# The opening of a diffusion trunk: the first norm's row by one product with ones, its root by logarithm and exponential, and another order of the first loads

## The chip, the cores and the metric

The kernel runs on one core of one Trainium2 chip. The metric is the device time of one execution in microseconds; three runs of the kernel before gave 2091.67, 2094.18 and 2094.89 us. A core has TensorE (PE; its weight loads are listed as PEld), VectorE (DVE), ScalarE (ACT), GpSimd (POOL) and SyncE (SP). Each works through its own list of instructions strictly in order, and they wait for each other through semaphores. Transfers are issued from a queue (SP's or ACT's) and run on 16 DMA engines that all queues share.

## The reference

One layer of a trunk over 1024 latent tokens of width 1024 and 256 context tokens: a SwiGLU block, a mixing block (retention and gated linear attention), a second SwiGLU block, and a last norm. What matters here is the start of the first block:

```python
def rms_norm(x, w):
    y = xf * lax.rsqrt(jnp.mean(xf * xf, axis=-1, keepdims=True) + EPS)
    return (y * w.astype(jnp.float32)).astype(x.dtype)
...
m_l = jnp.split(cond_lat @ ada_w[i] + ada_b[i], N_MOD, axis=-1)
x = x + 0.5 * m_l[2][:, None, :] * swiglu(modulate(rms_norm(x, norm1_w[i]), m_l[0], m_l[1]),
                                            ffn1_w1[i], ffn1_w3[i], ffn1_w2[i])
```

`cond_lat` is silu(c), `modulate(h, shift, scale)` is h * (1 + scale) + shift.

## The kernel before

**Layout.** Activations lie with the width on the partitions: x is 16 tiles `x{tg}{k}` of 128 x 512, k = 0..7 the slice of the width, tg = 0, 1 the half of the tokens. Every float32 product is made of three fast ones: each operand is split into a high part (a rounding copy, on ACT) and a low part (the difference, on DVE), and high x high, high x low and low x high are summed in PSUM. For the activation the parts are `hh` and `hl`; for a weight `wh`, `whi`, `s` (high) and `wl`, `wlo`, `s` (low).

**The opening** is written out by hand in `first1`: on PE, DVE and ACT the program order is the order of execution. It loads x's first half (`load_x`), then weights (`raw`, by `fetch`) and columns of the modulation matrix (`ada`, 128 x 1024, by `pe_load`), all on SP's queue. The constants `cols`, `ident` and `ccol` (the conditioning as columns, padded with zeros to blocks of 32) come through ACT's queue.

The norm needs, for each token, one over the root of the mean square, in the same row on every partition. Before: `squares` sums the eight squared tiles into `nacc` (squares on ACT, adds on DVE; `nsq` has two buffers); `rstd_col` multiplies `nacc` with ones on PE, which gives a column for each 128 tokens; `pow_half` takes the power -0.5 (a scale and shift on DVE, the power on GpSimd); `rows_diag` makes four diagonal matrices on DVE; `rstd_rows` multiplies ones with them on PE, which gives the row in PSUM (`pr`), and a copy `nrb`.

Each tile k also needs two columns of modulation: scale, number 8 + k, and shift, number k. In the opening the first few are made on PE: `pe_sums` (eight narrow products of `ccol` with an `ada` tile), a copy `csum` on ACT, `pe_turn` (a product that brings the partial sums to the partitions), and `pe_out` on ACT into `mod`; scale columns then pass `mod_fin` on DVE. The rest of the scale columns are sums of products on DVE (`mod_sum`, tile `junk`), with the conditioning spread to all partitions (`condc`), to which `cond_silu` applies silu on ACT.

With row and columns, tile k is normed: x times scale times row on DVE (`norm_a1`, or the first half of `norm_a`), `hh` on ACT with the shift (`norm_a2`), `hl` on DVE (`norm_b`).

**The steps.** Six weight blocks i = 0..5 are multiplied side by side. In step st (0 to 7) PE does three products for each block with tile k = st, 18 in all, and in between the column sum and turn for tile st + 1. While it does, ACT and DVE norm tile st + 1 and split further weights (`FIRST` says which in which step), SP loads the second half of x (`X1`), and ACT and DVE square and add it (`SQ`). In step 7 the second half's `rstd_col` comes, and soon after its row. Before the norm is ready, `warm` keeps PE busy with products of ones, in the numbers of `WARM`.

**Tables.** ACT's functions sit in sets that are loaded. At the start a silu on a small tile (`warm` in `run`) brings in the silu set.

Of the kernel before, what the change touches and what calls it, by code (L numbers as in the profile page):

```python
# [390 lines left out]
class Trunk:  # L391
# [36 lines left out]
    def consts(self):  # L428
        nc, I, cp = self.nc, self.I, self.cp
        self.cols = self.tile(cp, [P, I["cols"].shape[1]], F32, "cols")  # L430
        nc.scalar.dma_start(self.cols, I["cols"])
        self.pad(cp, 16)
# [5 lines left out]
        nc.vector.memset(self.mhalf, -0.5)  # L438
        self.mods = self.tile(cp, [P, 112], F32, "mod")
        self.mod = [self.mods[:, :72], self.mods[:, 72:]]  # L440
# [16 lines left out]
    def pe_cond(self, pool):  # L457
        nc = self.nc
        t = self.tile(pool, [P, 36 * KD], F32, "ccol")[:, :33 * KD]
        nc.scalar.dma_start(t, self.I["ccol"])  # L460
        self.sel = t[:, 32 * KD:32 * KD + 2]
        self.ccol = t[:, :32 * KD]
        nc.scalar.activation(self.ccol, self.ccol, AF.Silu)
# [669 lines left out]
    def first1(self, pools, n1):  # L1133
# [25 lines left out]
        def load(i, q):  # L1159
            low(i, q, high(i, q))  # L1160
# [21 lines left out]
        x0, x1 = self.x[0], None  # L1182
        self.ndg, idle, pss, acc = 4, self.psA(), {}, None
# [21 lines left out]
        self.norm_a(0, 0, a, b, pr, n1, x0[0])  # L1205
        rb[0] = self.scr(n1, "nrb")
        nc.scalar.copy(rb[0], pr)
        low(1, 0, raw)
        sm = self.pe_copy(pc, P, n1)
# [4 lines left out]
        o9 = self.pe_turn(rc, 4, sm[0])  # L1214
        for i in range(2):
            mms(i, 0, (1,))
        load(2, 0)
        self.pe_out(9, o9)
        load(3, 0)
        self.norm_a1(0, 1, a, rb[0], x0[1])  # L1220
        self.pe_sums(pc, P, cur[1])
        raw = high(4, 0)
        sm = self.tile(n1, [P, P], F32, "csum128", 2)
        nc.scalar.copy(sm, pc[:, P:2 * P])
        low(4, 0, raw)
        load(5, 0)
        cur = {}
# [3 lines left out]
        for i in range(2, 6):  # L1231
            if i == 4:
                o1 = self.pe_turn(rc, 6, sm)
                self.pe_out(1, o1)
                self.norm_a2(0, 1, b, x0[1])
            pss[i] = (self.psA if i < 4 else self.psB)()
            mms(i, 0, (0, 2, 1))
        self.norm_b(0, 1, b, x0[1])
        self.cond_silu()
        for st in range(1, KD):  # L1240
            n = st + 1
            for w in FIRST.get(st, ()):
                fetch(*w)
            if st in X1:
                self.load_x(pools, (1,), X1[st])
            if n + 2 < KD:
                cur[10 + n], cur[n + 2] = self.mod_load(10 + n), self.pe_load(n + 2)
            if st == KD - 2:
                w3 = [self.tile(self.dp, [P, D], F32R, f"ada{i}") for i in (1, 2, 3, 4)]
                ws += [[tuple(t[:, o:o + 512] for t in w3[j:j + 2]) for o in (0, 512)] for j in (0, 2)]  # L1250
            for i in range(6):
                mms(i, st, (0, 2, 1))
                if i == 0 and n < KD:
                    sm = sums(n, 0)
                    self.mod_sum(8 + n, cur.pop(8 + n), (0,), True)
                    self.norm_a1(0, n, a, rb[0], x0[n])
                if i == 2 and n < KD:
                    self.pe_out(n, self.pe_turn(pc, 2 * P, sm))
                    self.norm_a2(0, n, b, x0[n])
                    self.norm_b(0, n, b, x0[n])  # L1260
                    for w in FIRST.get(st, ()):
                        load(*w)
                    if st in SQ:
                        acc = self.squares(self.x[1], 512, n1, "", SQ[st], acc)
                if n == KD:
                    if i == 0:
                        self.c_silu(0, 0, pss[0], True)
                        load(6, 0), load(6, 1)
                    if i == 2:
                        r = self.rstd_col(acc, 512, n1)  # L1270
                        self.c_mul(0, 0, pss[1])
                        self.c_silu(1, 0, pss[2], True)
                    if i == 4:
# [25 lines left out]
    def load_x(self, pools, tgs, ks=tuple(range(KD))):  # L1299
        nc, I = self.nc, self.I  # L1300
        for tg in tgs:
            o, n = TGS[tg]
            self.x.setdefault(tg, [])
            for k in ks:
                t = self.tile(pools[tg], [P, n], F32, f"x{tg}{k}")
                src = I["xT"][k * P:(k + 1) * P, o:o + n] if tg < 2 else I["ctxT"][k * P:(k + 1) * P, :]
                nc.sync.dma_start(t, src)
                self.x[tg].append(t)
# [639 lines left out]
    def run(self):  # L1948
# [18 lines left out]
        warm = self.tile(self.dp, [P, 64], F32, "warm")[:, :8]  # L1967
        nc.scalar.activation(warm, self.mhalf, AF.Silu)
# [48 lines left out]
        for at, (tg, k) in zip(xat, ((tg, 4 * q + k) for tg, q in ((0, 0), (1, 1), (0, 1), (1, 0)) for k in range(4))):  # L2017
            o = TGS[tg][0]
            plan[at].append(lambda tg=tg, k=k, o=o: nc.sync.dma_start(self.x[tg][k], I["xT"][k * P:(k + 1) * P, o:o + 512]))
# [204 lines left out]
for _n, _w in (("ada_b", 72), ("norm1_w", 8), ("norm2_w", 8), ("norm3_w", 8), ("final_norm_w", 8),  # L2224
               ("ret_norm_w", 4), ("gla_norm_w", 4), ("gla_b", 4)):
# [9 lines left out]
def layout(inputs):  # L2235
# [3 lines left out]
    A["xT"] = c(g["x"][0].T)  # L2239
# [5 lines left out]
    A["ccol"] = np.zeros((P, 33 * KD), np.float32)  # L2245
    for i, n in enumerate(("c", "c_ctx")):
        A["ccol"][:, i:32 * KD:32] = g[n].reshape(KD, P).T
        A["ccol"][i::32, 32 * KD + i] = 1.0
# [69 lines left out]
```

## Time and profile before

| | us |
|---|---|
| median of three runs | 2094.18 |
| the profiled execution | 2095.94 |
| its span on the core | 2094.1 |
| TensorE busy | 2079.5 |
| VectorE busy | 1464.5 |
| ScalarE busy | 965.7 |
| GpSimd busy | 198.0 |
| start of the first product of hh with a weight | 18.66 |

A timeline row reads: start, duration (of all in the row, from the first's start to the last's end), engine, line, operation, output<-inputs, partitions x elements, how many, and in brackets the idle time just before and what ended it. A float32 product of 128 x 128 with ones shows as two records. A row of a table of stretches reads: stretch, length, then busy time and count of PE, PEld, DVE, ACT and POOL, TensorE's granted clock, the share of the DMA engines, GB/s. A row of waits names who waited for whom, the total, the number and the longest. PE's records overlap (each carries its pipeline's run-out), so the spacing of starts is the better measure there.

### The profile page before, as it was taken

Reading aid. Unit: us, or ns where it says so; the run is one execution under the profiler, and the core shown is the slowest. Engines: PE = TensorE matmul, PEld = TensorE weight load, DVE = VectorE, ACT = ScalarE, POOL = GpSimd, SP = SyncE. Lnnn points to the kernel's source line nnn. Section 1 sums busy time; section 2 is a strip of 40 time slices with the busy share of each in tenths; the row PEclk is TensorE's granted clock in tenths of the full one; section 3 lists DMA queues with packets and bytes.
Section 4 is the critical chain, followed back from the end, with each engine's and each line's share of the span. In section 5 each row is a group of like instructions: output and inputs, shape, how many; then the busy total and the mean of one; then the engine's idle time right before and its main releaser. Section 6 shows DMA issues by size and latency. Waiting matters only on the chain.

```text
span 2094.1 us, 34655 instructions
## 1 busy us (share of the span) xinstructions
PE 2079.5 (99%) x12646; PEld 1782.1 (85%) x12646; DVE 1464.5 (70%) x2649; ACT 965.7 (46%) x1806; POOL 198.0 (9%) x196
## 2 busy tenths in 40 slices
PE   9999999999999999999999999999999999999998
PEld 7888888888889999999789988888788888888888
DVE  6889999666775445863786368768766666665686
ACT  5433433435544445665664246444434334344552
POOL 0000000000015664001011001000000000010000
PEclk9999999999999999999999999999999999999999
DMA  9267767459886553663222223242344454477674
GB/s 347 86 232 236 241 219 253 151 164 367 287 293 217 181 182 103 207 207 91 88 76 85 76 81 104 91 161 81 106 160 140 144 170 156 148 237 231 219 241 142
DMA packets 199643, 366.54 MB, mean 175 GB/s; under 512 B 23216, under 2 KB 36400, under 8 KB 199472
## 3 DMA queue, kind: packets, MB, share of 16 engines
q1 hardware_dynamic: 199040, 364.07, 52.7%
q8 instruction: 99, 1.62, 0.3%
q14 instruction: 72, 0.59, 0.1%
q10 hardware_dynamic: 432, 0.26, 0.0%
HBM read 289.66 MB, written 66.19 MB: 170 GB/s over the span
## 4 chain that ended last, share of the span: by engine, by line
PE 89%; DVE 4%; DMA 4%; issue 1%; ACT 1%; SPq 0%; DVEq 0%; POOL 0%; POOLq 0%; ACTq 0%
PE psa L147 18%; PE psa L424 11%; PE psa L426 11%; PE psa L425 11%; PE psb L426 9%; PE psb L425 9%; PE psb L424 9%; PE psb L147 8%; DMA raw<-in_w 1%; PE psa L1174 1%; DVE wlo L420 1%; DMA hl<-sd 1%; PE psa L1168 1%; DVE junk L505 1%; DMA s<-in_w 1%
## 5 line engine op out<-in xcount | busy, mean ns | idle before, releaser
L419 ACT ACTIVATE whi<-raw 128x512 fp32r<-128x512 f32 x371 | 234.0, 631 | 504.0 <-issue 155.0
L420 DVE TENSOR_TENSOR wlo<-raw,whi 128x512 fp32r<-128x512 f32 x371 | 255.2, 689 | 175.3 <-ACT whi L419 174.6
L424 PE MATMUL psa<-hh,whi 128*128 128x512 f32 x684 | 266.8, 390 | 0.1
L425 PE MATMUL psa<-hl,whi 128*128 128x512 f32 x684 | 266.2, 389 | 0.0
L426 PE MATMUL psa<-hh,wlo 128*128 128x512 f32 x684 | 266.2, 389 | 0.0
L425 PE MATMUL psb<-hl,whi 128*128 128x512 f32 x568 | 221.3, 390 | 0.9 <-DVE hl L420 0.9
L426 PE MATMUL psb<-hh,wlo 128*128 128x512 f32 x568 | 221.2, 390 | 0.6 <-DVE wlo L420 0.6
L424 PE MATMUL psb<-hh,whi 128*128 128x512 f32 x568 | 221.2, 389 | 0.5 <-ACT whi L419 0.5
L147 PE MATMUL psa<-hl,whi 128*128 128x512 f32 x384 | 153.5, 400 | 0.0
L147 PE MATMUL psa<-hh,whi 128*128 128x512 f32 x384 | 152.5, 397 | 0.0
L147 PE MATMUL psa<-hh,wlo 128*128 128x512 f32 x384 | 152.4, 397 | 0.0
L424 PEld LDWEIGHTS psa<-hh,whi 128*128 128x128 f32 x684 | 128.4, 188 | 27.4 <-ACT s L720 0.6
L426 PEld LDWEIGHTS psa<-hh,wlo 128*128 128x128 f32 x684 | 128.3, 188 | 26.8 <-DVE wlo L420 0.2
L425 PEld LDWEIGHTS psa<-hl,whi 128*128 128x128 f32 x684 | 128.4, 188 | 26.2
L147 DVE TENSOR_TENSOR wlo<-raw,whi 128x512 fp32r<-128x512 f32 (+1 forms) x132 | 83.0, 645 | 93.4 <-ACT whi L147 91.2
L420 POOL TENSOR_TENSOR hl<-s,hh 128x512 fp32r<-128x512 f32 x88 | 132.2, 1529 | 144.7 <-DVE hl L420 80.7
L147 ACT ACTIVATE whi<-raw 128x512 fp32r<-128x512 f32 (+1 forms) x132 | 77.5, 598 | 121.5 <-PE psa L147 101.2
L425 PEld LDWEIGHTS psb<-hl,whi 128*128 128x128 f32 x568 | 106.6, 188 | 24.2 <-DVE hl L420 2.2
L426 PEld LDWEIGHTS psb<-hh,wlo 128*128 128x128 f32 x568 | 106.6, 188 | 23.5 <-DVE wlo L420 1.5
L424 PEld LDWEIGHTS psb<-hh,whi 128*128 128x128 f32 x568 | 106.6, 188 | 23.3 <-ACT whi L419 1.0
L426 PE MATMUL psa<-hh,hl 128*128 128x256 f32 x392 | 111.1, 284 | 0.0
L424 PE MATMUL psa<-hh,hh 128*128 128x256 f32 x392 | 111.1, 283 | 0.0
(414 smaller groups left out, 4919.5 us busy)
## 6 DMA issues: line engine op xcount, KB each, us to landing
raw<-in_w SPq DMA_DIRECT2D x242, 256.0 KB, 3.4
s<-in_w SPq DMA_DIRECT2D x198, 256.0 KB, 3.8
gd<-s SPq DMA_DIRECT2D x154, 256.0 KB, 2.8
ada<-in_adaT SPq DMA_DIRECT2D x60, 512.0 KB, 4.4
raw<-gd SPq DMA_DIRECT2D x91, 256.0 KB, 3.1
sd<-s SPq DMA_DIRECT2D x44, 256.0 KB, 2.7
raw<-sd SPq DMA_DIRECT2D x44, 256.0 KB, 3.4
hh<-in_w SPq DMA_DIRECT2D x44, 256.0 KB, 3.8
```

Of the source, the lines that this page charges most:

```text
L147: self.rec.add(self.eng, lambda: f(*map(get, a), **{x: get(v) for x, v in k.items()}), outs, ins, name, a, k)
L419: nc.scalar.activation(hi, src, AF.Copy)
L420: (eng or nc.vector).tensor_tensor(out=lo, in0=src, in1=hi.bitcast(F32), op=ALU.subtract)
L424: mm(ps, wa[0], xa[0], start=start, stop=False, skip_group_check=more)
L425: mm(ps, wa[0], xa[1], start=False, stop=False, skip_group_check=more)
L426: mm(ps, wa[1], xa[0], start=False, stop=stop, skip_group_check=more)
L505: nc.vector.tensor_tensor_reduce(out=self.junk, in0=t, in1=self.cs[s], scale=1.0, scalar=self.col("ada_b")[:, j:j + 1], op0=ALU.mult, op1= ...
L1168: nc.tensor.matmul(idle[:, :P], self.ones, self.ones, start=True, stop=True)
L1174: nc.tensor.matmul(pss[i], w[u], h[v], start=k == 0 and j == 0, stop=k == KD - 1 and j == js[-1])
```

## The change

Six things change, all before step 7 ends.

- The row of the first norm is one product of a matrix of ones with `nacc`, 512 wide, which leaves each token's sum on every partition. ACT then takes the logarithm of (sum / 1024 + EPS) and the exponential of -0.5 times it. `rstd_col`, the power, the diagonals and their products are no longer used for this norm (they still are for the second half's).
- ACT starts with the set that holds logarithm and exponential. The silu of the conditioning columns becomes x / (1 + exp(-x)): one exponential on 16 columns and three DVE operations; `ccol` is zeroed on DVE and no longer loaded, the conditioning and `sel` come with `cols`, now 134 wide instead of 116. The silu set is loaded later, at `cond_silu`.
- `ident` moves from ACT's queue to SP's, behind the first weights.
- SP loads in another order: four weights, then column 9, two weights, column 1. Column sums 8 and 0 are each copied, turned and written in turn, after the row's product; the sums of 9 and 1 move into step 0.
- x's halves lie contiguous in memory.
- Numbers: `WARM` (32, 3, 4) instead of (40, 2, 4); the loads and squares of x's second half come later (`X1`, `SQ`), with two of the squares in step 7, whose `rstd_col` is one block later; in step 1 the sums come two blocks later.

```diff
     def consts(self):
-        nc.scalar.dma_start(self.ident, I["ident"])
+        self.eps = self.tile(cp, [P, 8], F32, "eps")
+        nc.vector.memset(self.eps, EPS)
...
     def pe_cond(self, pool):
-        t = self.tile(pool, [P, 36 * KD], F32, "ccol")[:, :33 * KD]
-        nc.scalar.dma_start(t, self.I["ccol"])
-        nc.scalar.activation(self.ccol, self.ccol, AF.Silu)
+        self.sel = self.col("sel")
+        self.ccol = self.tile(pool, [P, 32 * KD], F32, "ccol")
+        nc.vector.memset(self.ccol, 0.0)
+        e, x = self.tile(pool, [P, 16], F32, "cexp"), self.col("conds")
+        nc.scalar.activation(e, x, AF.Exp, scale=-1.0)
+        nc.vector.tensor_scalar(out=e, in0=e, scalar1=1.0, scalar2=None, op0=ALU.add)
+        nc.vector.reciprocal(e, e)
+        i2 = lambda t: t.rearrange("p (i k) -> p k i", i=2)
+        nc.vector.tensor_tensor(out=self.ccol.rearrange("p (k r) -> p k r", r=32)[:, :, :2], in0=i2(x), in1=i2(e), op=ALU.mult)
...
     def first1(self, pools, n1):
-        n1r = self.rstd_col(self.squares(x0, 512, n1), 512, n1, w=P, ps=rc)
-        fetch(0, 0), fetch(1, 0)
-        cur.update({j: self.pe_load(j) for j in (9, 1)})
-        for i in range(2, 6):
-            fetch(i, 0)
-        self.pe_sums(pc, 0, cur[8]), self.pe_sums(pc, P, cur[0])
-        sm = self.pe_copy(pc, 2 * P, n1)
-        raw = high(0, 0)
-        warm(WARM[1])
-        dg = [self.rows_diag(n1r, i, n1) for i in range(4)]
-        o = [self.pe_turn(rc, 2 * i, sm[i]) for i in range(2)]
-        self.pe_out(8, o[0]), self.pe_out(0, o[1])
-        low(0, 0, raw)
-        self.rstd_rows(n1r, 512, n1, dg=dg, pr=pr)
-        raw = high(1, 0)
-        self.pe_sums(pc, 0, cur[9])
+        for w in ((0, 0), (1, 0), (2, 0), (3, 0)):
+            fetch(*w)
+        cur[9] = self.pe_load(9)
+        fetch(4, 0), fetch(5, 0)
+        cur[1] = self.pe_load(1)
+        nc.sync.dma_start(self.ident, self.I["ident"])
+        nc.tensor.matmul(pr, self.ones, self.squares(x0, 512, n1), start=True, stop=True)
+        rb[0] = self.scr(n1, "nrb")
+        nc.scalar.activation(rb[0], pr, AF.Ln, bias=self.eps[:, 0:1], scale=1.0 / D)
+        nc.scalar.activation(rb[0], rb[0], AF.Exp, scale=-0.5)
+        sm = []
+        for i, j in enumerate((8, 0)):
+            self.pe_sums(pc, i * P, cur.pop(j))
+            sm.append(self.tile(n1, [P, P], F32, "csum128", 2))
+            nc.scalar.copy(sm[i], pc[:, i * P:(i + 1) * P])
+            warm(WARM[1])
+            self.pe_out(j, self.pe_turn(rc, 2 * i, sm[i]))
         warm(WARM[2])
+        load(0, 0)
+        self.norm_a(0, 0, a, b, rb[0], n1, x0[0])
+        load(1, 0)
         self.norm_b(0, 0, b, x0[0])
...
             for i in range(6):
                 mms(i, st, (0, 2, 1))
-                if i == 0 and n < KD:
+                if i == 2 * (st == 1) and n < KD:
                     sm = sums(n, 0)
...
                 if n == KD:
                     if i == 0:
                         self.c_silu(0, 0, pss[0], True)
+                        acc = self.squares(self.x[1], 512, n1, "", SQ[st], acc)
                         load(6, 0), load(6, 1)
                     if i == 2:
-                        r = self.rstd_col(acc, 512, n1)
...
+                    if i == 3:
+                        r = self.rstd_col(acc, 512, n1)
...
-        warm = self.tile(self.dp, [P, 64], F32, "warm")[:, :8]
-        nc.scalar.activation(warm, self.mhalf, AF.Silu)
+        nc.scalar.preload_act_table_set("natural_log_exp_and_others")
...
-X1 = {3: range(4), 4: range(4, 6), 5: range(6, 8)}
-SQ = {4: range(4), 5: range(4, 6), 6: range(6, 8)}
-WARM = (40, 2, 4)
+X1 = {3: range(2), 4: range(2, 5), 5: range(5, 8)}
+SQ = {5: range(3), 6: range(3, 6), 7: range(6, 8)}
+WARM = (32, 3, 4)
...
-    A["xT"] = c(g["x"][0].T)
+    A["xT"] = c(g["x"][0].reshape(2, 512, D).transpose(0, 2, 1))
```

How the instructions move. First ACT around the first norm, before, from the copy of the column sums (`csum`) to the first `hh`; `wh` is the first weight's high part, `mod` the modulation columns.

```order
L478 COPY csum_83_273<-psb_166 128x256
L1153 ACTIVATE wh_153<-raw_241 128x512
L486 ACTIVATE mod_88<-psb_164,cols_78 128x2 x2
L1153 ACTIVATE whi_296<-raw_243 128x512
L596 ACTIVATE hh_18_119<-x_9_91,mod_88 128x512
```

Now, with the logarithm and exponential (`nrb`) ahead:

```order
L1201 ACTIVATE nrb_248<-psb_169,eps_87 128x512
L1202 ACTIVATE nrb_248<-nrb_248 128x512
L1207 COPY csum_84_259<-psb_170 128x128
L491 ACTIVATE mod_89<-psb_168,cols_78 128x2
L1207 COPY csum_85_275<-psb_170 128x128
L491 ACTIVATE mod_89<-psb_168,cols_78 128x2
L1158 ACTIVATE wh_157<-raw_207 128x512
L601 ACTIVATE hh_19_123<-x_9_91,mod_89 128x512
L1158 ACTIVATE whi_290<-raw_209 128x512
```

The copies and columns are single now, `wh` has moved from ahead of the columns to behind both, and the second weight's `whi` from ahead of `hh` to behind it. On DVE at the same place the order is kept, now without the diagonals: `mod_fin`, the low part `wl`, then the norm, then `wlo` and `hl`.

```order
L537 SCALAR_TENSOR_TENSOR mod_89<-mod_89,cols_78 128x1
L1162 TENSOR_TENSOR wl_158<-raw_207,wh_157 128x512
L600 SCALAR_TENSOR_TENSOR x_9_91<-x_9_91,mod_89,nrb_248 128x512
L1162 TENSOR_TENSOR wlo_291<-raw_209,whi_290 128x512
L612 SCALAR_TENSOR_TENSOR hl_20_124<-x_9_91,mod_89,hh_19_123 128x512
```

What moved there is only what the rows wait for. Last, ACT from the last `hh` of the first half into step 7 of the change; `nsq` are squares of x's second half, `s` the first silu, `ada` the split of a later weight.

```order
L608 ACTIVATE hh_33_137<-x_16_105,mod_89 128x512
L560 ACTIVATE nsq_648<-x_132_530 128x512
L560 ACTIVATE nsq_651<-x_133_532 128x512
L560 ACTIVATE nsq_654<-x_135_569 128x512
L725 ACTIVATE s_669<-psa_295 128x512
L560 ACTIVATE nsq_671<-x_136_571 128x512
L560 ACTIVATE nsq_674<-x_137_573 128x512
L1158 ACTIVATE ada_142_618<-raw_677 128x512
```

Before, two squares stood between the last `hh` and the silu, and none behind it.

More of the change, by code (lines that the diff above doesn't have):

```diff
@@ L1180, in sums @@
             return sm
[L1182 to L1183 removed]
+        x0, acc = self.x[0], None
+        self.ndg, idle, pss = 4, self.psA(), {}
         rc, pr, pc = self.psB(), self.psB(), self.psB()
@@ L1213, in first1 @@
             mms(i, 0, (0, 2))
-        o9 = self.pe_turn(rc, 4, sm[0])
+        load(2, 0)
         for i in range(2):
             mms(i, 0, (1,))
-        load(2, 0)
-        self.pe_out(9, o9)
         load(3, 0)
[L1220 to L1227, printed above, removed]
+        sm = sums(9, 0)
+        for i in range(2, 6):
+            pss[i] = (self.psA if i < 4 else self.psB)()
+            mms(i, 0, (0, 2, 1))
+            if i == 2:
+                self.pe_out(9, self.pe_turn(rc, 4, sm))
+                self.norm_a1(0, 1, a, rb[0], x0[1])
+                load(4, 0)
+            if i == 3:
+                load(5, 0)
+                sm = sums(1, P)
+            if i == 4:
+                self.pe_out(1, self.pe_turn(rc, 6, sm))
+                self.norm_a2(0, 1, b, x0[1])
+                self.norm_b(0, 1, b, x0[1])
         self.cond_load()
```

37 lines of the change are left out of this document (10 added, 27 removed).

## The prediction

> **What bounds the kernel now.** Read first were the page and the table of stretches, to see where TensorE is short of work.
>
> ```profile
> PE 2079.5 (99%) x12646; PEld 1782.1 (85%) x12646; DVE 1464.5 (70%) x2649; ACT 965.7 (46%) x1806; POOL 198.0 (9%) x196
> 0.00:62.00 62.00, 60.52 (x444) 49.20 (x445) 42.30 (x79) 33.01 (x68) 2.38 (x8) 1.00 0.86 311
> 62.00:100.00 38.00, 38.00 (x173) 31.62 (x172) 32.80 (x53) 15.97 (x26) 0.00 (x0) 1.00 0.24 85
> ```
>
> From 62 us on PE has no gap left to close, and the order of every engine from there on is the old one, so a shift of PE at 62 us should reach the end whole. PE's 60.52 busy us before it hide that much of it is idle warming. So I read the timeline of the opening; columns are start, duration, engine, line.
>
> ```profile
> 0.72 5.00 SPq L1307 DMA_DIRECT2D x<-in_xT  x8
> 1.04 11.97 PE L1168 MATMUL psa<-ones 128*128 128x128 f32 x80 [1.04 <-DVE mhalf L438]
> 7.26 3.11 DVE L556 TENSOR_TENSOR nacc<-nacc,nsq 128x512 f32<-128x512 f32 x4 [0.87 <-ACT nsq L555]
> 9.95 1.35 ACT L555 ACTIVATE nsq<-x 128x512 f32<-128x512 f32 x2 [0.51 <-DMA x<-in_xT]
> 10.61 1.49 DVE L556 TENSOR_TENSOR nacc<-nacc,nsq 128x512 f32<-128x512 f32 x2 [0.24 <-ACT nsq L555]
> 12.84 1.06 PE L565 MATMUL psb<-ones,nacc 128*128 128x128 f32 x8
> 15.24 0.63 ACT L1153 ACTIVATE wh<-raw 128x512 fp32r<-128x512 f32 x1
> 15.87 1.14 PE L581 MATMUL psb<-ndiag,ones 128*128 128x128 f32 x8
> 16.04 0.42 ACT L486 ACTIVATE mod<-psb,cols 128x2 f32<-128x2 f32 x2 [0.17 <-PE psb L482]
> 16.42 0.68 DVE L1157 TENSOR_TENSOR wl<-raw,wh 128x512 fp32r<-128x512 f32 x1
> 17.04 0.75 DVE L595 SCALAR_TENSOR_TENSOR x<-x,mod,psb 128x512 f32<-128x512 f32 x1
> 17.89 0.72 ACT L596 ACTIVATE hh<-x,mod 128x512 fp32r<-128x512 f32 x1 [0.91 <-DVE x L595]
> 18.66 0.50 PE L1174 MATMUL psa<-hh,wh 128*128 128x512 f32 x1
> ```
>
> The sum of squares is ready at 10.61 + 1.49 = 12.10, but PE takes it when its warming ends at 13.01. From there a chain PE, DVE, POOL, DVE, PE, DVE, ACT leads to the first real product at 18.66. In that chain the two modulation columns (two sums, two turns) and the first weight's high part (15.24) lie beside the power and the diagonals; that matters below.
>
> **The change, part by part.** Let T be the start of the new product with ones.
>
> *When T comes.* The last loads of x sit behind a wait:
>
> ```profile
> SPq L1307 <- DMA cols<-in_cols: 1.4, 1, 1.4
> ```
>
> A later load of x waited until `cols` had landed. With ident and ccol off ACT's queue only the eighth load of x has to wait so, and less is moved ahead of it. DVE's adds then bind: four in 3.11 us, 0.76 each. I estimate the third tile's add 0.5 us earlier than 7.26, six adds of 0.76 from there: 11.3. The bounds are 11.0 (adds from the first tile on without a gap) and 12.1 (x lands as before). Eight warm products fewer are 16 of 80 records; they end near 11.2. I take T = 11.35.
>
> *From T to the first product.* The prices:
>
> ```profile
> 18.98 0.27 ACT L478 COPY csum<-psb 128x128 f32<-128x128 f32 x1
> 19.47 0.42 PEld L482 LDWEIGHTS psb<-ccol,csum 128*128 128x128 f32 x2
> 19.70 0.28 PE L482 MATMUL psb<-ccol,csum 128*128 128x2 f32 x2
> 20.01 0.26 ACT L486 ACTIVATE mod<-psb,cols 128x2 f32<-128x2 f32 x1 [0.23 <-PE psb L482]
> 20.48 0.64 PE L473 MATMUL psb<-ada,ccol 128*32 128x128 f32 x16
> 17.51 1.16 PE L1168 MATMUL psa<-ones 128*128 128x128 f32 x8
> 1260.71 0.69 ACT L147 ACTIVATE t<-psb,cols 128x512 f32<-128x512 f32 x1
> 1261.43 1.29 ACT L147 ACTIVATE t<-t 128x512 f32<-128x512 f32 x2
> ```
>
> The product of 512 columns has no row; L565 and L581, as many columns in four pieces, bound it at 1.06 and 1.14. Logarithm and exponential (the pair at 1260.71 has the same shapes) take 0.69 + 0.65. So the row is ready at T + 2.45, where the old way needed 17.01 - 13.01 = 4.0: 1.5 us won, and the power, four diagonals and their products gone. But ACT now carries both, and the columns come behind: csum(8) from T + 2.4 to 2.67, its turn 0.51 (19.47 to 19.98) to 3.24, mod(8) to 3.53; only then sums(0), 0.6, to 3.84; copy to 4.15, three warm products (0.27 each, from L1168) until 4.64, turn to 4.95, mod(0) to 5.24. On ACT `wh` stands behind mod(0): 5.13 to 5.76. On DVE `wl` stands before the first norm: 5.80 to 6.48. Then x 6.42 to 7.17, hh 7.27 to 7.99, first product at T + 8.04 = **19.4, against 18.66: +0.7**. With T at its bounds: +0.4 to +1.5.
>
> *Steps 0 to 6.* A step is 18 products, one column sum and one turn; undisturbed it takes 39.76 - 34.63 = 5.13.
>
> ```profile
> 24.16 0.40 PE L1174 MATMUL psa<-hh,wh 128*128 128x512 f32 x1
> 34.63 0.39 PE L1174 MATMUL psa<-hh,wh 128*128 128x512 f32 x1
> 39.76 0.39 PE L1174 MATMUL psa<-hh,wh 128*128 128x512 f32 x1
> 23.79 1.14 ACT L455 ACTIVATE condc<-condc 128x512 f32<-128x512 f32 x2
> 24.96 1.28 DVE L505 CUSTOM_DVE_ANT_0 junk<-ada,condc,cols 128x1024 bf16<-128x1024 f32 x1 [0.29 <-ACT condc L455]
> 998.52 1.28 ACT L147 ACT_TABLE_LOAD   x1
> 999.82 0.60 ACT L147 ACTIVATE sg<-psa 128x512 f32<-128x512 f32 x1
> 45.21 2.29 DVE L556 TENSOR_TENSOR nacc<-nacc,nsq 128x512 f32<-128x512 f32 x3 [0.29 <-ACT nsq L555]
> 50.55 0.50 PE L1174 MATMUL psa<-hh,wh 128*128 128x512 f32 x1 [0.38 <-ACT hh L603]
> 56.12 0.39 PE L1174 MATMUL psa<-hh,wh 128*128 128x512 f32 x1
> ```
>
> Counted from the first product: sums(9), formerly in the norm's shadow, now lies in step 0 (+0.6). The second weight's `whi` stands behind hh on ACT (to 0.5), its low part before `hl` on DVE (to 1.25), `hl` ends at 1.95; so the first six products take 2.4 instead of some 1.55 (+0.85). Then sums(9) to 3.0, third weight to 3.7, turn(9), fourth weight to 4.7, sums(1) to 5.3. ACT does mod(9) to 4.35, DVE the norm of tile 1 to 5.3 and only then the fifth weight's low part, to 6.0, which PE wants at 5.53 (+0.45). turn(1) ends at 6.75, mod(1) at 7.05, hh(1) at 7.8, PE is free at 7.4 (+0.4); hl(1) is another 0.35 late, against 0.1 before (+0.25). Together +1.1. The new table load, 1.30 to the next instruction, delays the silu of `condc`; junk, x, hh and hl of step 2 follow, and the sums moved two products later hide all but 0.2. On the other side, the three steps from 39.76 to 56.12 took 16.36 where 3 x 5.13 is 15.39: the adds that held DVE there are spread and come later, -0.95. Sum **+1.8**, between +1.2 (splits ready in time) and +2.4.
>
> *Step 7.*
>
> ```profile
> 56.40 1.48 DVE L556 TENSOR_TENSOR nacc<-nacc,nsq 128x512 f32<-128x512 f32 x2
> 57.07 0.60 ACT L720 ACTIVATE s<-psa 128x512 f32<-128x512 f32 x1 [0.34 <-PE psa L1174]
> 58.26 0.95 PE L565 MATMUL psb<-ones,nacc 128*128 128x1 f32 x8
> ```
>
> Here nacc was ready at 57.88, 0.38 ahead of PE. Now three adds follow hl(7) and two more squares stand behind the first silu, with two nsq buffers. With 0.74 an add and 0.6 a square or silu, counted from the step's start: the three adds run from 0 to 2.1 (the third square waits for a buffer until the first add is done), ACT's silu from 1.27 to 1.87, the last squares to 2.4 and 2.98 (again behind buffers), the last add to 3.85. PE wants nacc after four groups of three products, at 2.83: it stalls **1.1**. Behind it the reciprocal root and diagonals on DVE are late by a further 0.25: **+1.35**, between +0.5 (adds done 0.8 sooner) and +2.0.
>
> *Free edits.* The five small DVE operations for `ccol` end before x's second square; ident is next read in step 7; x's halves contiguous are the same 256 KB in the same 128 rows; the mid-kernel reloads of x are not waited for by PE in any row read.
>
> Sum: 0.7 + 1.8 + 1.35 = 3.85 us. The profiled execution took 2095.94 (span 2094.1 and 1.84 around it), so it would take 2099.8; the runs shown have their median 1.76 lower, which gives **2098.0**.
>
> [...]
>
> **The rivals.**
> 1. *The norm's row was the bound.* Were the columns ready with the row, the first product would come at row + 0.06 + 0.75 + 0.10 + 0.72 + 0.06, T + 4.1; with T = 11.0 that is 15.1, 3.5 us sooner, and with the stalls gone (-0.4) the kernel ends at 2090.2; were only `wl` out of the way, 2091.4. For it speaks that this row was the end of the old chain; against it, that ACT and DVE are strictly in order and `wh` stands behind mod(0). Chance 0.22.
> 2. *PE cools down.* The warm-up shows two paces:
>
> ```profile
> 2.00:4.00 2.00, 2.00 (x12) 2.00 (x11) 0.00 (x0) 1.13 (x2) 0.00 (x0) 1.00 0.90 260
> 10.00:12.00 2.00, 2.00 (x20) 2.00 (x20) 1.66 (x3) 1.21 (x2) 0.00 (x0) 1.00 1.02 377
> ```
>
> Some 6 us at the pace of 12, not 20, cost up to 6 x 0.4 = 2.4 us. The new gap ahead of the first product is from the last warm products, T + 6.0, to T + 8.04, 2 us; no such gap stands in the trace before. Time 2100.4. [...] Together 0.20. [...]
> 3. *The late squares cost nothing*, since DVE, freed of the old stalls, runs ahead in step 6: the third term falls away and 2096.6 remains. 0.06.
>
> **How the numbers follow.** Forecast 0.52, its own range 2096.4 to 2099.7. A difference of 0.2% is 4.2 us, about what a measurement of this kernel can tell. The forecast lies just inside it (the bound is 2098.4), so about half of its own range, 0.26, is slower by more. Slower: 0.26 + 0.20 = 0.46. Faster: 0.14 of the first rival's 0.22, whose 2090.2 is close above the bound of 2090.0 and would fall below it with any reserve that I have not seen in x's loads. Same: 0.26 + 0.08 + 0.06 = 0.40. The range reaches from the first rival's 2090.5 to 2101.0, above the second's; about 0.18 is left out.
>
> **What would show it.** The product with ones starts at 11.0 to 12.1; the first product of hh not before 18.5, its releaser hh, hh's the norm, with `wl` just before it on DVE; the row nrb done 3 us or more before DVE reads it. Step 1 starts 7.8 us after the first product instead of 5.5. PE waits about 1 us for nacc in step 7. A first product at 16 us, or step 7 without a stall, would prove the first or third term wrong; matmul rows slowed after the gap, the second rival.

## The result, and the profile after

The changed kernel takes **2104.11 us** (median of six runs, 2103.57 to 2106.73); six runs of the kernel before have the median 2095.01 (2091.67 to 2096.21). The ratio is 1.0049, with a 95% interval of 1.0039 to 1.0058: 9.1 us slower. The forecast was 3.85 us slower, 2098.0, with a range up to 2101.0: the direction was called, and some 5 us were missing. The runs below were taken in four jobs, and the medians of the kernel before differ by up to 2.3 us between jobs and this result. So each run is compared with the runs of before in its own job: the ratio is to these, and its 95% interval stands in brackets.

First the page of the profile after, its row of the engines, and from the table of stretches the two that were shown of before:

```profile
PE 2082.3 (99%) x12624; PEld 1775.1 (84%) x12624; DVE 1463.3 (70%) x2649; ACT 968.5 (46%) x1808; POOL 203.1 (10%) x195
```

```profile
0.00:62.00 62.00, 56.36 (x404) 42.47 (x404) 37.92 (x69) 32.40 (x65) 0.36 (x6) 1.00 0.83 299
62.00:100.00 38.00, 37.35 (x171) 30.85 (x172) 32.99 (x56) 18.77 (x32) 1.39 (x1) 1.00 0.20 65
```

DVE and ACT are as busy as before over the span (1463.3 against 1464.5, 968.5 against 965.7); PE is busy 2.8 us longer in a span that is 8.1 longer (2102.2 against 2094.1). To see what the opening costs, the timeline of after, PE first:

```profile
10.95 1.13 PE L1199 MATMUL psb<-nacc,ones 128*128 128x512 f32 x2 [0.86 <-DVE nacc L561]
...
15.47 1.14 PE L1173 MATMUL psa<-ones 128*128 128x128 f32 x8
18.68 0.50 PE L1179 MATMUL psa<-hh,wh 128*128 128x512 f32 x1 [2.07 <-ACT hh L601]
...
19.93 0.49 PE L1179 MATMUL psa<-hh,wlo 128*128 128x512 f32 x1 [0.23 <-DVE wlo L1162]
20.59 0.50 PE L1179 MATMUL psa<-hl,wh 128*128 128x512 f32 x1 [0.17 <-DVE hl L612]
...
26.80 0.50 PE L1179 MATMUL psa<-hh,wh 128*128 128x512 f32 x1 [0.31 <-ACT hh L608]
...
58.54 0.39 PE L1179 MATMUL psa<-hh,wh 128*128 128x512 f32 x1
...
62.65 1.05 PE L570 MATMUL psb<-ones,nacc 128*128 128x1 f32 x8 [1.21 <-DVE nacc L561]
...
65.05 0.39 PE L424 MATMUL psa<-hh,ada 128*128 128x512 f32 x1
```

and ACT and DVE ahead of the first product, and DVE in step 7:

```profile
12.11 0.69 ACT L1201 ACTIVATE nrb<-psb,eps 128x512 f32<-128x512 f32 x1 [2.15 <-PE psb L1199]
12.83 0.63 ACT L1202 ACTIVATE nrb<-nrb 128x512 f32<-128x512 f32 x1
...
15.81 0.62 ACT L1158 ACTIVATE wh<-raw 128x512 fp32r<-128x512 f32 x1
17.91 0.72 ACT L601 ACTIVATE hh<-x,mod 128x512 fp32r<-128x512 f32 x1 [1.48 <-DVE x L600]
```

```profile
16.46 0.69 DVE L1162 TENSOR_TENSOR wl<-raw,wh 128x512 fp32r<-128x512 f32 x1 [1.92 <-ACT wh L1158]
17.07 0.74 DVE L600 SCALAR_TENSOR_TENSOR x<-x,mod,nrb 128x512 f32<-128x512 f32 x1
...
58.72 3.87 DVE L561 TENSOR_TENSOR nacc<-nacc,nsq 128x512 f32<-128x512 f32 x5
```

The row of the norm is done at 13.46, and DVE reads it at 17.07: it lies ready for 3.6 us while columns, `wh` and `wl` pass, as forecast. The row at 65.05 is the first product behind step 7. In the kernel before that row stands at 61.24:

```profile
61.24 0.39 PE L424 MATMUL psa<-hh,ada 128*128 128x512 f32 x1
```

So the opening, up to this row (called L424 below), loses **3.81 us**; the forecast had 3.85. The rest is behind it, where the order of PE's work is the old one. There, rows of after from a stretch of plain products show two paces:

```profile
1700.63 0.39 PE L424 MATMUL psb<-hh,whi 128*128 128x512 f32 x1
...
1703.35 0.40 PE L424 MATMUL psb<-t1h,whi 128*128 128x512 f32 x1
...
1706.15 0.40 PE L424 MATMUL psb<-t2h,whi 128*128 128x512 f32 x1
```

From 1700.63 to 1703.35 lie twelve products with `hh` or `hl` as the moving tile, 2.72 us or 0.2267 each; from 1703.35 to 1706.15 twelve with `t1`, 2.80 us or 0.2333 each, with no wait on any of them; the rows are 0.39 or 0.40 us long and overlap. In the kernel before twelve products with `t2` take 2.72 us:

```profile
1701.25 0.39 PE L424 MATMUL psb<-t2h,whi 128*128 128x512 f32 x1
...
1703.97 0.39 PE L424 MATMUL psb<-hh,whi 128*128 128x512 f32 x1
```

So a product with `t1` is 3% slower in the change, and no wait in the profile shows it. The simplest gauge of it is the count of PE's records in 300 us where PE never pauses; before, then after:

```profile
1550.00:1850.00 300.00, 300.00 (x1325) 248.47 (x1325) 203.06 (x333) 119.19 (x208) 0.00 (x0) 1.00 0.45 153
```

```profile
1550.00:1850.00 300.00, 300.00 (x1308) 245.10 (x1307) 201.01 (x330) 116.00 (x202) 0.00 (x0) 1.00 0.45 152
```

17 records fewer at 0.2267 are 3.9 us lost in this stretch, at the same granted clock of 1.00 and the same DMA share. Read by the moving tile (named first in a row's inputs; the weights come second), the slow products are those with x (110 to 460 us; 0.2325 on average against 0.2270 in the kernel before) and with t1 to t3 of the second block (1450 to 1860; 0.2333).

### The profile page after: what moved, and what is told of

It is laid out like the page before. It is cut to its first block, busy times and chain, and to the rows that moved or that the text cites. A ratio compares the mean times of both kernels' runs of the same rounds, so it can differ in the third digit from the quotient of the medians.

```text
span 2102.2 us, 34615 instructions
## 1 busy us (share of the span) xinstructions
PE 2082.3 (99%) x12624; PEld 1775.1 (84%) x12624; DVE 1463.3 (70%) x2649; ACT 968.5 (46%) x1808; POOL 203.1 (10%) x195
## 4 chain that ended last, share of the span: by engine, by line
PE 92%; DMA 3%; DVE 3%; ACT 1%; issue 1%; SPq 0%; DVEq 0%; POOL 0%; POOLq 0%; ACTq 0%
PE psa L147 18%; PE psa L424 12%; PE psa L426 12%; PE psa L425 12%; PE psb L425 9%; PE psb L426 9%; PE psb L424 9%; PE psb L147 8%; DMA raw<-in_w 1%; PE psa L1179 1%; DMA raw<-gd 1%; DVE nacc L561 0%; DVE wlo L420 0%; DVE hl L420 0%; PE psb L1179 0%
## 5 line engine op out<-in xcount | busy, mean ns | idle before, releaser
L424 PE MATMUL psa<-hh,whi 128*128 128x512 f32 x684 | 266.8, 390 | 0.0
L424 PE MATMUL psb<-hh,whi 128*128 128x512 f32 x568 | 221.3, 390 | 0.7 <-ACT whi L419 0.5
L424 PEld LDWEIGHTS psa<-hh,whi 128*128 128x128 f32 x684 | 128.4, 188 | 27.6 <-ACT s L725 0.4
L420 POOL TENSOR_TENSOR hl<-s,hh 128x512 fp32r<-128x512 f32 x88 | 138.1, 1596 | 136.4 <-DVE hl L420 80.4
L424 PEld LDWEIGHTS psb<-hh,whi 128*128 128x128 f32 x568 | 106.6, 188 | 24.1 <-ACT whi L419 1.0
L424 PE MATMUL psa<-hh,hh 128*128 128x256 f32 x392 | 110.5, 282 | 0.0
```

What stands on the lines that cost most here:

```text
L420: (eng or nc.vector).tensor_tensor(out=lo, in0=src, in1=hi.bitcast(F32), op=ALU.subtract)
L424: mm(ps, wa[0], xa[0], start=start, stop=False, skip_group_check=more)
```

## The experiments

What differs there between the kernels is where the tiles lie in SBUF, the on-chip memory; the program's tiles are allotted from its left and from its right end. The change widens `cols` from 116 to 134 columns, the pad among the constants from 16 to 20, and adds `eps`: every tile on the left side of SBUF (normed input, weights) moves up by 128 bytes. Without the `warm` tile, x of the opening moves up by 256 bytes on the right side. The built programs allot, in bytes within a partition:

| | before | after |
|---|---|---|
| `hh00` (left) | 3200 | 3328 |
| `whi`, first buffer (left) | 81024 | 81152 |
| `x00` of the opening (right) | 169600 | 169856 |
| `t1h0` of the second block (right) | 163712 | 163712 |
| `x00` - `whi`, modulo 256 | 0 | 128 |
| `t1h0` - `whi`, modulo 256 | 0 | 128 |
| `hh00` - `whi`, modulo 256 | 0 | 0 |

The slow products are those whose distance is 128 here. Theory A says that the addresses make the pace, B that the shift in time does, and C that the loads do. Two later theories split A: by A1 it is the distance of moving tile and weights, taken modulo 256 bytes, by A2 the place of the left tiles by itself.

**Addresses put back in the change.**

```diff
-        self.pad(cp, 20)
...
-        self.eps = self.tile(cp, [P, 8], F32, "eps")
+        self.eps = self.mhalf[:, 4:]
...
+        self.pad(self.dp, 64)
```

> The change, with two things put back that no step of the prediction had costed: the constants take the room that they had (no pad, the bias of the logarithm in the unused half of mhalf), and 64 columns are set aside again where the warm tile lay. So every tile that TensorE reads lies where it lay in the kernel before; no instruction of TensorE, VectorE or ScalarE differs from the change. Theory A (the 3.8 us that the opening loses are the whole of the mechanism that was predicted, and the other 5 us are a slower pace of products that goes with the addresses of the tiles): about 2098.8 us, 3.8 over the kernel before, and the mean spacing of the 128x512 products is back at 0.227 us between 100 and 470 us and between 1450 and 1850 us, where the change has 0.2283 and 0.2290 to 0.2309. Theory B (the pace comes from the shift in time, by which transfers and other engines fall elsewhere beside the products): 2104 us, the spacing as in the change. Theory C (the contiguous loads of x or the other loads slow TensorE): 2104 us too.

2099.96 us (2098.80 to 2101.59), before 2093.87; ratio 1.0027 [1.0016, 1.0038]. The count is back:

```profile
1550.00:1850.00 300.00, 300.00 (x1325) 248.42 (x1324) 203.15 (x334) 118.70 (x207) 0.00 (x0) 1.00 0.44 155
```

So A holds, against B and C: the order of every engine is the change's, and the old pace is back. Of the 9.1 us over the kernel before, 6.1 are left. That is more than the 3.8 of the opening; the profile of this run loses another 2.2 us there (below, at the gap ahead of the first product).

**The kernel before with its left side 128 bytes higher.**

```diff
-        self.pad(cp, 16)
+        self.pad(cp, 48)
```

> The kernel before with its pad among the constants 48 columns wide and not 16: every tile of the left side of SBUF lies 128 bytes higher, as in the change, and nothing else differs on any engine but the pad's own memset. Theory A, where the addresses of the normed input, the weights and the t tiles make the pace: 2097 to 2100 us, 2 to 5 over the kernel before, with the slower spacing (0.229 to 0.231 us) between 1450 and 1850 us, where both operands lie on the left side; the part between 100 and 470 us may need the other shift too. Theories B and C: 2095 us, no difference.

2098.90 us (2097.69 to 2100.74), before 2093.87; 1.0024 [1.0015, 1.0033]. One number in the program costs 5.0 us, and the count is the slow one:

```profile
1550.00:1850.00 300.00, 300.00 (x1307) 245.13 (x1307) 201.29 (x329) 116.69 (x203) 0.00 (x0) 1.00 0.43 150
```

The part between 100 and 470 us did not need the other shift: the mean spacing from 100 to 150 us, worked out from the starts of neighbouring products, is 0.2291 against 0.2267 in the kernel before.

**The kernel before with x of the opening 256 bytes higher.**

```diff
-        warm = self.tile(self.dp, [P, 64], F32, "warm")[:, :8]
+        warm = self.warm[:, :8]
```

(`self.warm` is the pad's tile.)

> The kernel before with its 64-column warm tile taken out of the right side of SBUF (the first activation writes into the pad): the tiles of x of the opening lie 256 bytes higher, as in the change, all else is the same. Theory A: if the address of x alone makes the slower pace between 100 and 470 us, about 2096.5 us (0.0014 us on each of some 1600 products), and no difference after 500 us; if only the relation of x to the weights does, it may go either way by as much. Theories B and C: 2095 us, no difference.

2093.32 us, before 2093.87; 0.9997 [0.9989, 1.0006]. No difference, and no slower spacing: the expected 2096.5 was a miss. A shift of x by 256 bytes does nothing and one of the left side by 128 does all, which is what led to A1.

**Both sides, and the right side alone, by 128.** The right side is moved by the pad at its end, `self.pad(edge, 24)` made 56; the first run has the wider pad on the left as well.

> The kernel before with the left side of SBUF 128 bytes higher (as in the run that cost 5 us) and the right side 128 bytes lower, so that tiles of the two sides keep their distance but for a multiple of 256 bytes. Theory A1 (what counts is the distance of a product's moving tile and its weights, taken modulo 256 bytes): 2094 us, no difference, and the spacing of the 128x512 products back at 0.2267 us from 1550 to 1850 us. Theory A2 (what counts is where the left tiles, the weights among them, lie by themselves): 2099 us, the spacing at 0.2295 to 0.2300 us there.

> The kernel before with only the right side of SBUF 128 bytes lower; the left side, with all weights, lies where it lay. Theory A1: 2099 us as if the left side had been moved, the spacing 0.2295 to 0.2300 us from 1550 to 1850 us and about 0.2285 between 100 and 450 us, and the stretch from 600 to 870 us some 2 us shorter as there. Theory A2: 2094 us, no difference.

Both sides: 2093.38 us, before 2093.94; 0.9999 [0.9990, 1.0008]. Right side alone: 2100.38; 1.0029 [1.0018, 1.0040]. The counts, in this order:

```profile
1550.00:1850.00 300.00, 300.00 (x1326) 248.39 (x1325) 204.13 (x334) 119.46 (x207) 0.00 (x0) 1.00 0.44 153
```

```profile
1550.00:1850.00 300.00, 300.00 (x1308) 245.16 (x1307) 201.39 (x330) 117.25 (x203) 0.00 (x0) 1.00 0.44 150
```

A1 holds in both and A2 in neither: with every weight where it was, moving the other side costs as much (6.4 us by the medians, with an interval that overlaps the one of the left side), and moving both costs nothing.

**The same on the change.** Only `self.pad(edge, 24)` becomes 56.

> The change itself with one number altered: the pad at the right end of SBUF is 56 columns wide and not 24, so that the right side lies 128 bytes lower, as the left side lies 128 higher; no other instruction differs. Theory A1 (the distance of moving tile and weights modulo 256 bytes sets the pace): as the run with the old addresses, 2099 to 2100.5 us, with 0.2267 us between the 128x512 products from 1550 to 1850 us, though every address is another than in the kernel before. Rivals (the shift in time, the loads, or absolute addresses): 2104 us.

2099.47 us (2097.02 to 2101.06), before 2092.72; 1.0031 [1.0019, 1.0043], and the count is 1326:

```profile
1550.00:1850.00 300.00, 300.00 (x1326) 248.39 (x1325) 204.45 (x336) 118.77 (x207) 0.00 (x0) 1.00 0.44 154
```

Moving the other side as well brings the old pace back, as putting everything back did, with every address another than before.

**The late squares.** On the kernel with the old addresses, `X1`, `SQ` and the places of `rstd_col` and of these loads are those of before:

```diff
-X1 = {3: range(2), 4: range(2, 5), 5: range(5, 8)}
-SQ = {5: range(3), 6: range(3, 6), 7: range(6, 8)}
+X1 = {3: range(4), 4: range(4, 6), 5: range(6, 8)}
+SQ = {4: range(4), 5: range(4, 6), 6: range(6, 8)}
```

> The change with the old addresses and, in addition, the second group's squares, their loads and the reduction of their sum (L570 in the change) where the kernel before has them: a step earlier, with the reduction after the product that opens step 7's third group. Theory P (the prediction: the late sum of squares stalls TensorE 1.1 us in step 7 and 0.25 us more at the diagonals): 1.2 to 1.4 us under the run with old addresses alone, about 2098.6 us, with no wait of TensorE on nacc in step 7. Rival: TensorE waits as long a little later for the next late thing (the step's own products are bound by the loads), and the time stays at 2100 us. In single executions the clock granted after the first idle gap may add 2 us to either.

2098.80 us (2096.38 to 2100.15), before 2093.94; 1.0021 [1.0012, 1.0030]. It is 1.16 under the run with the old addresses (another job; against the kernel before, 4.9 in place of 6.1), close to the expected 1.2 to 1.4. PE takes nacc in step 7 without a wait; rows of step 7's start, the reduction, and the first product behind it:

```profile
60.91 0.39 PE L1178 MATMUL psa<-hh,wh 128*128 128x512 f32 x1
...
63.01 0.95 PE L569 MATMUL psb<-ones,nacc 128*128 128x1 f32 x8
...
65.95 0.39 PE L424 MATMUL psa<-hh,ada 128*128 128x512 f32 x1
```

Step 7 is 65.95 - 60.91 = 5.04 us here and 65.05 - 58.54 = 6.51 in the change.

**The gap ahead of the first product.** The run with the old addresses should have lost 3.81 us up to L424, and lost 67.41 - 61.24 = 6.17. Here is the stretch from 19 to 27 us in the change, in that run, and in the run with old squares:

```profile
19.00:27.00 8.00, 7.16 (x55) 4.17 (x54) 4.89 (x9) 4.25 (x11) 0.00 (x0) 1.00 0.96 358
```

```profile
19.00:27.00 8.00, 7.77 (x47) 4.53 (x46) 4.45 (x8) 2.87 (x7) 0.00 (x0) 0.57 0.84 317
```

```profile
19.00:27.00 8.00, 7.48 (x49) 4.34 (x49) 4.67 (x8) 3.12 (x8) 0.00 (x0) 0.79 0.81 305
```

The column behind POOL's is the granted clock: 1.00, 0.57 and 0.79. All three have the same gap ahead of the first product, 2.07 or 2.08 us. So idle products were put into the gap, on the kernel with old squares:

```diff
-WARM = (32, 3, 4)
+WARM = (32, 3, 11)
```

> The run with old squares, with eleven idle products ahead of the first real one and not four, so that TensorE's gap before it (2.07 us there) all but closes; the seven more end before the first product's data. Theory K (the rival of the prediction that was put as PE cooling down: after that gap the granted clock falls in some executions, to 0.57 between 19 and 27 us in one run and 0.79 in another, and costs 1.5 to 2.3 us there): the granted clock is 1.00 in every stretch of the opening, step 1 starts 8.1 us after the first product and not 9.6, and the median falls by 1 to 1.5 us to about 2097.5 with its highest run lower. Rival: the lower clock has another cause (the load of the chip, the start of the program): still a stretch under 1.00 in the profile or the same median, 2098.8 us.

2096.57 us, before 2093.74; 1.0016 [1.0007, 1.0025]; 2.2 under the run with old squares, more than the 1 to 1.5 expected. Nine of its ten runs lie between 2095.98 and 2097.75, one at 2100.42. Its first product and the clock:

```profile
18.71 0.50 PE L1178 MATMUL psa<-hh,wh 128*128 128x512 f32 x1 [0.51 <-ACT hh L600]
```

```profile
19.00:27.00 8.00, 7.15 (x55) 4.14 (x55) 4.86 (x9) 4.24 (x11) 0.00 (x0) 1.00 0.94 357
```

From first product to L424 it takes 45.70 us, with old squares 47.17, both with the same instructions: at the lower clock it took 1.5 longer. With the old addresses alone it took 2.2 longer than in the change (48.61 against 46.37), and in the change with its right side down 0.9 (47.30).

The profile of the kernel before has such a fall too, to 0.51, far behind the opening and after a shorter gap of 1.36 us:

```profile
1022.25 0.41 PE L147 MATMUL psb<-ident,t 128*128 128x128 f32 x2 [1.36 <-DVE t L147]
```

```profile
1024.00:1027.40 3.40, 3.40 (x42) 2.74 (x41) 2.58 (x6) 3.27 (x8) 0.00 (x0) 0.51 0.52 174
```

In the change the products with `ident` follow without this gap, but one of 1.38 us stands just ahead, before the 64x32 products at 1021.60; the granted clock from 1021 to 1027 us is 1.00 there, and no fall follows before the end. So spans of single profiles, 2102.2 against 2094.1, are not the cost of the change to a microsecond.

**Another order of the opening.** Two runs, on the kernel with old addresses and old squares. In the first the weight is split ahead of the logarithm, and both column sums follow the row's product and are copied together:

```diff
+        load(0, 0)
         nc.tensor.matmul(pr, self.ones, sq, start=True, stop=True)
...
+        self.pe_sums(pc, 0, cur.pop(8)), self.pe_sums(pc, P, cur.pop(0))
+        sm = self.pe_copy(pc, 2 * P, n1)
```

> The run with old squares, with the opening's chain put in another order: the first weight is split before the logarithm, the two sums of the modulation columns follow the product with ones at once and are copied together, their turns follow, and the second weight's high part comes after them. Theory P (the first real product waits for the columns, the first weight and then the normed tile, one behind the other, on ScalarE and VectorE): the first product comes at 16.6 to 17.2 us in place of 18.7, the gap of TensorE before it shrinks under 1 us, and the time falls by 1.5 to 2 us to 2096.5 to 2097. Rival 1: the later weights and the next columns hold step 1 where it was (26.8 us), so the gain is lost there and the time stays near 2098.6. Rival 2: weights have not landed when the first split asks for them, which holds the logarithm behind it on ScalarE: the first product at 18.5 us or later, no gain.

2094.50 us, before 2093.94; 1.0001 [0.9992, 1.0009]: 4.3 under the run with old squares, not 1.5 to 2; under the run with the gap filled (another job), whose clock stayed at 1.00 as well, it is 2.1. The first product came at 17.75, later than hoped, since the split waited 2.48 us for its weight to land, as the second rival had it, and the logarithm with it. But step 1 came at 24.89, and not at 28.40 (26.83 where the gap was filled and the clock kept), and the gap of 1.15 us left the clock at 1.00 in the profile. The second run puts the split behind the logarithm and the exponential last, fills the gap, and takes column 1 one product group earlier:

```diff
         nc.scalar.activation(rb[0], pr, AF.Ln, bias=self.eps[:, 0:1], scale=1.0 / D)
+        raw = high(0, 0)
+        self.pe_sums(pc, 0, cur.pop(8)), self.pe_sums(pc, P, cur.pop(0))
+        sm = self.pe_copy(pc, 2 * P, n1)
         nc.scalar.activation(rb[0], rb[0], AF.Exp, scale=-0.5)
```

> The run with an early row and early weights, changed once more: on ScalarE the logarithm, the first weight's high part, the copy of both column sums and only then the exponential (there the split waited 2.48 us for its weight to land, with the logarithm and exponential behind it); seven idle products keep TensorE busy; and column 1's sums and turn come one product group earlier in step 0. Theory P (the chain on ScalarE sets the first product): first product at 16.4 to 16.9 us in place of 17.75, step 1 near 23 us in place of 24.9, and 1.3 to 1.8 us less, about 2092.9 us, 1 us under the kernel before. Rival: weights and columns 9 and 1 land too late for so early a start, step 1 stays at 24.5 us or later and the time at 2094.5 us.

2092.23 us (2090.93 to 2095.12), before 2093.74; 0.9993 [0.9984, 1.0002], so not clear of the kernel before by its time. The first product comes at 16.39 and step 1 at 22.86, both as Theory P had them. ACT's rows of this run:

```profile
11.95 0.69 ACT L1201 ACTIVATE nrb<-psb,mhalf 128x512 f32<-128x512 f32 x1 [1.99 <-PE psb L1199]
12.69 0.63 ACT L1157 ACTIVATE wh<-raw 128x512 fp32r<-128x512 f32 x1
13.22 0.35 ACT L482 COPY csum<-psb 128x256 f32<-128x256 f32 x1
13.47 0.63 ACT L1205 ACTIVATE nrb<-nrb 128x512 f32<-128x512 f32 x1
14.27 0.42 ACT L490 ACTIVATE mod<-psb,cols 128x2 f32<-128x2 f32 x2 [0.17 <-PE psb L486]
```

`wh` and the copy lie where ACT otherwise waits for PE, and hh follows at 15.61 instead of 17.91. In the profile L424 comes at 59.97, 1.27 ahead of the kernel before.

**The context group's tiles.** In the stretch from 655 to 820 us products are 256 wide, and there the runs with one side moved were shorter. A pad of 32 columns above those tiles moves them alone:

```diff
+        gap = opn("gap", "right")
+        self.pad(gap, 32)
         hc = opn("hc", "right")
```

> The kernel before with 32 columns left free above the context group's tiles only, so that its 256-wide moving tiles (hh, hl, ghi, glo) lie 128 bytes lower in relation to their weights, and nothing else that TensorE reads moves. Theory A1 extended (in the stretch from 600 to 870 us the two runs with one side moved were about 2 us shorter, since 256-wide products go faster at the other distance): about 2092 us, 2 us under the kernel before, with all else as it was. Rival (that stretch was shorter for another reason, such as the s and raw tiles on the left against each other): 2094 us.

> The other opening together with the gap above the context tiles. If both act as put in their own runs, the gains add: about 2091 us, 3 us under the kernel before. If the opening's gain is lost later, or the gap does nothing: 2092 to 2094 us.

The pad alone: 2091.33 us, before 2093.74; 0.9992 [0.9983, 1.0001]. An interval that touches 1 settles nothing by itself, but the traces do. Two marks on ACT are the same two instructions in every kernel; in the kernel before, then here:

```profile
654.54 0.62 ACT L419 ACTIVATE whi<-s 128x512 fp32r<-128x512 f32 x1
...
820.40 0.42 ACT L419 ACTIVATE ghi<-s 128x256 fp32r<-128x256 f32 x1 [0.42 <-DVE s L966]
```

```profile
655.62 0.62 ACT L419 ACTIVATE whi<-s 128x512 fp32r<-128x512 f32 x1
...
819.80 0.42 ACT L419 ACTIVATE ghi<-s 128x256 fp32r<-128x256 f32 x1 [0.48 <-DVE s L966]
```

165.86 us against 164.18. Between these marks the runs with the distance 0 (both sides moved, x moved by 256, old addresses, the change with its right side down) took 165.86 or 165.87, and those with 128 (left side up, right side down, the change itself) 164.15 to 164.61. So the 256-wide products there gain 1.3 to 1.7 us by the distance that costs the 512-wide ones, and the pad earns that alone. The count of PE's records says the same, in the kernel before, then here:

```profile
705.00:805.00 100.00, 100.00 (x836) 100.00 (x835) 43.34 (x60) 51.40 (x102) 71.21 (x48) 1.00 0.54 177
```

```profile
705.00:805.00 100.00, 100.00 (x846) 100.00 (x845) 44.34 (x61) 51.44 (x102) 72.01 (x50) 1.00 0.52 177
```

PE never pauses in these 100 us and works off ten records more: the products are faster, and with this the extended A1 holds. With the other opening: 2091.40 us (2088.93 to 2093.55), 0.9988 [0.9979, 0.9997], the only interval that lies below 1. The stretch takes 164.17 where the other opening alone has 165.85; the median is 0.8 lower than that run's and 2.3 under the kernel before, where 3 was expected.

## Why the prediction was right and wrong

**The opening: right in kind, and close in sum by luck.** T was 10.95, just below the bound of 11.0, and the first product came at T + 7.73, not 8.04: +0.02 where 0.7 was forecast. Steps 0 to 6 lost 58.54 - 18.68 = 39.86 against 56.12 - 18.66 = 37.46 before, 2.4 where 1.8 was forecast; step 1 came 8.12 after the first product, where 7.8 was forecast, with the named waits (`wlo` 0.23, hh 0.31). PE stalled 1.21 on nacc in step 7, where 1.1 was forecast. The three terms were off by -0.7, +0.6 and less than 0.1; the sum is off by 0.04 because the first two cancel.

The 0.6 lies in steps 1 and 2. From 26.80 to 37.96 they took 11.16 us, and 10.47 before (24.16 to 34.63): 0.7 lost, where 0.2 was put for the new table load. Step 0 (2.6 lost) and the three steps with the adds (0.9 won) came nearly as forecast. The rows of the steps' starts and of DVE point at the load; no run leaves it out:

```profile
32.40 0.49 PE L1179 MATMUL psa<-hh,wh 128*128 128x512 f32 x1
...
37.96 0.39 PE L1179 MATMUL psa<-hh,wh 128*128 128x512 f32 x1
```

```profile
29.25 1.28 DVE L510 CUSTOM_DVE_ANT_0 junk<-ada,condc,cols 128x1024 bf16<-128x1024 f32 x1 [1.71 <-ACT condc L456]
...
32.37 0.75 DVE L612 SCALAR_TENSOR_TENSOR hl<-x,mod,hh 128x512 fp32r<-128x512 f32 x1 [0.85 <-ACT hh L608]
```

DVE waits 1.71 us for `condc`, which stands behind the load, and step 2's `hl` starts at 32.37, just as the step does at 32.40; in the kernel before it started 0.9 us ahead (28.59, the step at 29.50).

**The step that failed** is the paragraph on the free edits, and with it the sentence of the first part, "a shift of PE at 62 us should reach the end whole". That PE has no gap left was read from a row that ends at 100 us (a gap of 1.36 us ends at 1022), and where it holds it says only that PE's own pace sets the rest; that this pace stays the same was taken as given. The edits to `cols`, the pad, `eps` and `warm` were priced at nothing, if at all, and by their instructions. Their cost is the room that they take. By the run that moves only the left side it is 5.0 us, and 3.8 + 5.0 = 8.8 of the 9.1. The 5.0 are a difference of medians with an interval of some 3.1 to 6.9 us, so the 0.3 that are left mean nothing.

**The rivals.** That the norm's row was the bound fell: the row was ready 3.6 us early and the first product came at the old time. With columns and weight out of its way it does pay: the first product comes at 16.39 us in the other opening, where the rival had 15.1. (The range gives 2090.5 as this rival's time; its own paragraph has 2090.2.) That the late squares cost nothing fell: it is the run with old squares that is shorter, by 1.16. That PE cools down does not show in the profile of the change, whose granted clock from 19 to 27 us is 1.00. A lower granted clock does show in three other profiled executions with the same gap (0.57, 0.79, 0.79); from the first product to L424 they took 0.9 to 2.2 us longer than runs whose clock was 1.00, where 2.4 was the price. As the prediction says, the trace before has no gap of 2 us; but its rows at 1022 and 1024 show a fall after a shorter one. How often it fell in the runs of the change is not shown. No run shows the table load hold ACT longer than was put into steps 0 to 6: in the change it starts at 26.77 and the next instruction at 28.06, 1.29 us, where 1.30 was put.

## What to carry to other kernels

A change in a kernel that TensorE bounds can also change its tiles' addresses, and here 128 bytes on one side cost 5.0 us: compare the allotted addresses before and after, and the spacing of plain products in a stretch without waits, ahead of any theory on time. When a shared row of a norm is made faster, look at what else stands between it and the first product on the same in-order engines; here it paid only once the weight's split and the column copies lay in ScalarE's own waits. Try to fill an idle gap of TensorE even where the filling does no work: here a gap of 2.07 us, filled but for 0.51, was worth 2.2 us.

## What the runs showed of the hardware

**Distance of the operands.** A 128x512 product started every 0.2267 us where moving tile and weights lie a multiple of 256 bytes apart, and in the change every 0.2333 where they lie 128 bytes more; where both sides of the kernel before were moved by 128 bytes, the time stayed the same (2093.38 us against 2093.94). Only these two distances were tried, modulo 256, and no run shows why they differ. For the 256-wide products of the context group it was the other way round: 128 bytes more made their stretch 1.3 to 1.7 us shorter of 166.

**The clock after a short gap.** After a gap of 2.07 or 2.08 us the mean granted clock was 0.57 or 0.79 in the stretch from 19 to 27 us in three of the four profiled executions that have it, and 1.00 when the gap was 1.15 or 0.51. In the kernel before it was 0.51 for 3.4 us, soon after a gap of 1.36, and in the change 1.00 after one of 1.38 nearby. So the length of the gap alone does not decide it, and no run shows what else does.
